# Gate/up's weight sums partly by adding DMAs, and the wide weights' pool opened during the memory heads, in a two-layer encoder

## The chip, the cores and the metric

The kernel runs on 1 core of a Trainium2 chip. The metric is the device time of one execution in microseconds (us). TensorE (PE) multiplies, VectorE (DVE) and ScalarE (ACT) work element by element, GpSimd (POOL) and SyncE (SP) mostly issue DMA transfers here. Each engine works off its own instructions in order and waits for the others by semaphores.

## The reference

x has 512 tokens of width 1024. Two layers, each with a token mixer (latent attention in layer 0, grouped-query attention in layer 1) beside four cross-attention heads into 256 memory tokens, then a SwiGLU feed-forward of width 2816. All in float32.

```python
for i in range(DEPTH):
    h = _rmsnorm(x, norm_mix[i])
    ...
    mem_out = _memory_attention(q_mem, mem_n, w_mem_kv[i], memq_norm[i], memk_norm[i])
    x = x + jnp.concatenate([mix, mem_out], axis=-1) @ w_out[i]
    x = x + _swiglu(_rmsnorm(x, norm_ffn[i]), w_gate_up[i], w_down[i])

def _swiglu(h, w_gate_up, w_down):
    gu = h @ w_gate_up
    g, u = gu[..., :D_FF], gu[..., D_FF:]
    return (jax.nn.silu(g) * u) @ w_down
```

## The kernel before, in words

**Products.** Every product is made of three TensorE passes over operands split into a high and a low part (`mm3`, L135: lines 137, 138, 139 are high x high, high x low, low x high). A weight block is loaded raw by SyncE (`load_raw`, DMA at L166), cast to its high part `whi` by ScalarE (L154), and VectorE subtracts for the low part `wlo` (L155). TensorE's L137 needs `whi`, L138 needs `wlo`.

**Gate/up.** The product h @ [gate | up] is done for 6 groups of columns (g = 0 to 4 with 512 columns, g = 5 with 256), each as a 2 x 2 block product with 7 instead of 8 multiplications (Strassen-Winograd). The two halves of the contraction and gate, up give four weight blocks b11, b12, b21, b22 (tensors w_gu, w_gl; 512 KB a tile, two tiles a block in groups 0 to 4, one in group 5). The seven products run in the order P1, P7, P2, P5, P6, P4, P3. Their weights are built in place in the raw tiles by `prep` (L794), with four VectorE subtractions of 128 x 1024 a tile, all at L792 (`tadd`): two for P7, one for P6, one for P4; 88 in the program.

```python
if p == "P1":
    src = b11
elif p == "P7":
    tadd(b11, b12, b11)
    tadd(b12, b22, b12)
    src = b12
...
elif p == "P6":
    tadd(b11, b22, b11)
```

The activations' sums (S1 to S4) are made by `sums` (L703, instructions at L707), split at L249 (ACT) and L250 (DVE) into `op` tiles. `ahead` (L820) prepares each product's weights two steps before it is multiplied (CFG LW = 2). After P1 of group g, `act_T` (L852) transposes the finished activations of group g-1 on TensorE (16 `tp` of 128 x 128, L345, into two PSUM banks), and ScalarE copies them out (`at`, L860). `post` (L862) moves results from PSUM: copies of P1's (L867) and P7's (L871) by ScalarE.

**Order.** Attention and the memory heads run as streams that `merge` (L264) interleaves by the costs they yield; one of them is `out_prefix` (L661), the first part of the output projection `w_out` (L683), which begins while the last heads run. `pipe` (L285) runs the projections' heads and tails. Weight tiles come from one pool: narrow (512 columns, 6 buffers) while attention runs, wide (1024 columns, 3 buffers) from `weight_pool(True)` on, called after the merge in L1260 and L1400. Within an engine the scheduler of the framework then fixes the final order. POOL issues 10 small transfers in the whole program (L374, L375, L379).

Of the kernel before, what the change touches and what calls it, by code (L numbers as in the profile page):

```python
# [20 lines left out]
D = 1024  # L21
# [5 lines left out]
GRID_W = 64  # L27
THETA = 10000.0

CFG = dict(mid=3, mgap=3, mdel=7, warm=9, npre=(3, 3), pre=(6, 5), WC=512, mm=3, sc=3, tp=2, norm='VA', G=33, T=9,  # L30
           W=7, WH=6, WF=3, RF=3, PR=4, delay=12, ssq='AV', ahead=1, gtag=('sc', 'mm', 'mm', 'mm'), LA=3, wlos='V',
           wloa='V', wlof='V', wlod='V', scl='V', rm='V', rad='V', hi='A', rawe='A', LW=2, tadd='V',
           r=(0.534, 0.925, 0.95, 5, 1.124, 0.86, 1.362))
# [15 lines left out]
def encoder_kernel(ctx: ExitStack, tc: tile.TileContext, a: dict, out: bass.AP):  # L49
# [235 lines left out]
    def pipe(stages, delay=None):  # L285


        pend, mid = iter(()), []

        def small_steps(n):  # L290
            for _ in range(min(n, len(mid))):
                mid.pop(0)()

        for st in stages:
            head, tail = st[0], st[-1]
            c = 0.0
# [12 lines left out]
            mid = st[1] if len(st) == 3 else []  # L309
        small_steps(len(mid))  # L310
        yield from pend

    def run(g):
# [347 lines left out]
    def out_prefix(l, acts, banks, pre, n, tag, ready):  # L661


        while not ready():
            yield None
        banks += [bank(tag) for _ in range(n)]
        for kp in range(3):
            yield from out_block(banks, range(n), acts, kp, list(w_units(a["w_out"][l, 0, kp], 512)), kp == 0, False)
        pre.append(w_early(a["w_out"][l, 0, 3], 2))

    def x_T(X, k):

# [10 lines left out]
    def w_out(l, acts, banks, pre, X, g0, early):  # L683


        sq = small(8, f"sq{l}", bufs=1)
        R = [[g4((P, 2, 512), F32, "hr") for _ in range(2)] for _ in range(2)]
        rows = [[[r[:, :, h * 256 : (h + 1) * 256] for r in R[c]] for h in range(2)] for c in range(2)]
        tmp = {}

        def scale_rows(c):
            for k in range(4):
                A.mul(R[c][k // 2][:, k % 2], x_T(X, 4 * c + k), gcol(g0 + 4 * c + k))

        def operand(src):
            res = []
            for i in range(2):
                o = g4((P, 2, 2, 256), name="op")
                split((o[:, 0], o[:, 1]), src[i])
                res.append(o)  # L700
            return res

        def sums(x, y, op):  # L703
            o = g4((P, 2, 2, 256), F32, "hs")
            o = [o[:, i] for i in range(2)]
            for i in range(2):
                op(o[i], x[i], y[i])  # L707
            return o

        def get(name):  # L710
            (a11, a21), (a12, a22) = rows
            if name == "A11":
                return operand(a11)
            if name == "S3":
                return operand(sums(a11, a21, V.tensor_sub))
            if name == "A12":
                scale_rows(1)
                return operand(a12)
            if name == "S1":
                tmp["S1"] = sums(a21, a22, V.tensor_add)  # L720
                return operand(tmp["S1"])
            if name == "S2":
                tmp["S2"] = sums(tmp["S1"], a11, V.tensor_sub)
                return operand(tmp["S2"])
            if name == "A22":
                return operand(a22)
            return operand(sums(a12, tmp["S2"], V.tensor_sub))

        n = len(banks)
        steps = [(0, kp, range(4)) for kp in range(3, 6)]  # L730
        for kp in range(6):
            steps.append((1, kp, range(4)))
            if kp < 3:
                steps.append((0, kp, range(n, 4)))
        ws = list(pre)
        bs = [banks + [bank(OTAG[t]) for t in range(n, 4)], None]
        for i, (c, kp, ts) in enumerate(steps):
            for c2, kp2, _ in steps[len(ws) : i + 1 + CFG["LW"]]:
                ws.append(list(w_units(a["w_out"][l, c2, kp2], 512)))
            if i == 0 and l == 0:  # L740
                for t in range(4):
                    X[t] = g4(dt=F32, name="x")
                    nc.sync.dma_start(X[t], a["x"][t])
            if c == 1 and kp == 0:
                bs[1] = [bank(x) for x in ("sc", "sc", "mm", "mm")]
            if i + CFG["LW"] >= len(steps):
                early(get)
            for t in ts:
                late = c == 0 and t >= n
                run(out_block(bs[c], [t], acts, kp, ws[i], kp == (3 if late else 0), kp == (2 if late else 5)))  # L750
            if (c, kp) == (0, 5):
                add_x(X, 0, bs[0], sq, range(n))
            elif (c, kp) == (0, 2):
                add_x(X, 0, bs[0], sq, range(n, 4))
            elif (c, kp) == (1, 3):
                scale_rows(0)
        add_x(X, 1, bs[1], sq, range(4))

        def stats():
            tot = small(4, "sqt")  # L760
            V.tensor_add(tot, sq[:, :4], sq[:, 4:])
            return token_rstd(tot, 4, D, f"rf{l}")[0]

        return stats

# [5 lines left out]
    def ffn(l, X, acts, banks, pre, g0, emit):  # L771
# [11 lines left out]
        def ntile(g):  # L783
            return 2 if g < 5 else 1

        def load_q(g, q):
            if g < NG:
                src = [a["w_gu"][l, g, q, i] for i in range(2)] if g < 5 else [a["w_gl"][l, q]]
                raws[g, q] = [load_raw(x, 1024) for x in src]

        def tadd(o, x, y):
            (V if eng("tadd") == "V" else GP).tensor_sub(o, x, y)  # L792

        def prep(g, p, i):  # L794
            b11, b12, b21, b22 = [raws[g, q][i] if (g, q) in raws else None for q in range(4)]
            if p == "P1":
                src = b11
            elif p == "P7":
                tadd(b11, b12, b11)
                tadd(b12, b22, b12)  # L800
                src = b12
            elif p == "P2":
                src = b21
            elif p == "P5":
                src = b11
            elif p == "P6":
                tadd(b11, b22, b11)
                src = b11
            elif p == "P4":
                tadd(b11, b21, b11)  # L810
                src = b11
            else:
                src = b22
            return wsplit(src, 1024, "wlof")

        steps = [(g, p, i) for g in range(NG) for p in PROD for i in range(ntile(g))]
        ready = {}
# [2 lines left out]
        def ahead(n):  # L820
            while nprep[0] < min(n, len(steps)):
# [1 line left out]
                if g == i == 0:  # L823
                    ops[p] = getop[0](AOP[p])
                if i == 0:
                    for q in {"P1": [1, 3], "P7": [2], "P5": []}.get(p, []):
                        if (g, q) not in raws:
                            load_q(g, q)
# [17 lines left out]
        stats = w_out(l, acts, banks, pre, X, g0, early)  # L846
        st = {}

        def two():
# [12 lines left out]
        def post(g, p):  # L862
# [9 lines left out]
            elif p == "P2":  # L872
                st["gs"] = [pr(), pr()]
                for t in range(2):
                    A.activation(st["gs"][t][:, :n], st["A"][t], AF.Silu, scale=r[:, t : t + 1])
            elif p == "P5":
                st["p5"] = two()
                for t in range(2):
# [6 lines left out]
            elif p == "P4":  # L885
                for t in range(2):
                    w, z, q = [st[x][t][:, :n] for x in ("p1", "p5", "p7")]
                    V.tensor_add(q, st["B"][t], w)
                    A.activation(q, q, AF.Silu, scale=r[:, 2 + t : 3 + t])
                    V.scalar_tensor_tensor(z, z, r[:, 2 + t : 3 + t], q, ALU.mult, ALU.mult)  # L890
            else:
                for t in range(2):
                    w, q = st["p1"][t][:, :n], st["gs"][t][:, :n]
                    V.tensor_add(w, st["C"][t], w)  # L894
                    V.scalar_tensor_tensor(w, w, r[:, t : t + 1], q, ALU.mult, ALU.mult)  # L895
# [495 lines left out]
    for h in range(4):  # L1391
# [8 lines left out]
    weight_pool(True)  # L1400

    def emit1(c):
        pass
# [96 lines left out]
```

## Time and profile before

| | |
|---|---|
| runs | 1289.7, 1290.42, 1292.85 us (median 1290.42) |
| profiled execution | 1292.64 us, of it a span of 1290.5 us |
| busy: PE / DVE / ACT / POOL | 1268.8 / 936.5 / 698.7 / 6.2 us |
| granted clock of TensorE, mean | 0.996 of full |
| HBM read / written | 119.24 / 2.10 MB |
| L792: weight sums on DVE | 88, 105.7 us in all |

Busy time is the time in which an engine has an instruction under way; idle time is told by what ended it ("<-ACT whi L154": the engine waited until ScalarE wrote whi at line 154). The granted clock is the share of TensorE's full rate (2.4 GHz) that the throttle gave; half of it is 1.2 GHz. Matmuls overlap: one of 512 columns is shown with 0.39 us while the next starts 0.23 us after it. A count such as x4 behind a timeline row puts four instructions in a row together.

### The profile page before, as it was taken

The page shows a single profiled execution, that of the slowest core. Times are in us where ns is not written, and L with a number is a line of the kernel's source. Part 1 is how long each engine was busy: PE and PEld are TensorE (multiplying, and loading weights), DVE is VectorE, ACT ScalarE, POOL GpSimd, SP SyncE. Part 2 cuts the span into 40 slices and gives each one's busy share as a digit, 9 for nine tenths or more (in the row PEclk, how much of TensorE's full clock was granted, in tenths as well). Part 3 has the DMA queues.
Part 4 walks back from the last instruction along what each step waited for, and adds up shares of the span by engine and source line. Part 5 has one row for each costly group of instructions (what it writes and reads, how often), then busy time and mean ns, then how long its engine had stood idle before and what let it go on. Part 6 is the DMA issues. An engine that isn't in the chain of part 4 may idle for free. (4 is left out here: it accounts for less than half of the span.)

```text
span 1290.5 us, 17050 instructions
## 1 busy us (share of the span) xinstructions
PE 1268.8 (98%) x6425; PEld 1061.8 (82%) x6425; DVE 936.5 (73%) x1658; ACT 698.7 (54%) x1205; POOL 6.2 (0%) x17
## 2 busy tenths in 40 slices
PE   9999999999999999999999999999998999999998
PEld 6988878988778888988888888887876888898887
DVE  6699999846978988853336898965697888896221
ACT  5587766845655455552234568865474445555110
POOL 1000000000000000000000000000000000000000
PEclk9999999999999999999999999999999999999999
DMA  7342101052323231242223212131323223216110
GB/s 227 117 141 86 34 1 66 1 213 98 115 98 131 82 131 50 88 158 66 78 99 109 81 51 86 62 129 51 115 72 141 74 106 117 79 55 237 56 62 33
DMA packets 45457, 122.43 MB, mean 95 GB/s; under 512 B 5264, under 2 KB 9872, under 8 KB 45376
## 3 DMA queue, kind: packets, MB, share of 16 engines
q1 hardware_dynamic: 44784, 119.58, 26.8%
q0 software_dynamic: 592, 1.77, 0.4%
q8 instruction: 50, 0.82, 0.2%
q14 instruction: 31, 0.25, 0.1%
HBM read 119.24 MB, written 2.10 MB: 94 GB/s over the span
## 5 line engine op out<-in xcount | busy, mean ns | idle before, releaser
L155 DVE TENSOR_TENSOR wlo<-raw,whi 128x1024 fp32r<-128x1024 f32 (+3 forms) x342 | 343.7, 1013 | 235.7 <-ACT whi L154 233.7
L154 ACT CAST whi<-raw 128x1024 fp32r<-128x1024 f32 (+3 forms) x342 | 298.8, 885 | 395.7 <-PE sc L139 262.7
L137 PE MATMUL mm<-whi,g 128*128 128x512 f32 (+3 forms) x370 | 141.2, 382 | 1.2 <-ACT whi L154 1.2
L138 PE MATMUL mm<-wlo,g 128*128 128x512 f32 (+3 forms) x370 | 139.0, 376 | 0.5 <-DVE wlo L155 0.5
L139 PE MATMUL mm<-whi,g 128*128 128x512 f32 (+3 forms) x370 | 138.0, 376 | 0.0
L138 PE MATMUL mm<-wlo,op 128*128 128x512 f32 (+1 forms) x336 | 127.8, 380 | 4.3 <-DVE wlo L155 3.9
L137 PE MATMUL mm<-whi,op 128*128 128x512 f32 (+1 forms) x336 | 126.8, 377 | 4.8 <-ACT whi L154 4.5
L139 PE MATMUL mm<-whi,op 128*128 128x512 f32 (+1 forms) x336 | 126.4, 376 | 0.0
L138 PE MATMUL sc<-wlo,op 128*128 128x512 f32 (+1 forms) x336 | 125.7, 374 | 0.0
L139 PE MATMUL sc<-whi,op 128*128 128x512 f32 (+1 forms) x336 | 125.6, 374 | 0.0
L137 PE MATMUL sc<-whi,op 128*128 128x512 f32 (+1 forms) x336 | 125.2, 373 | 0.0
L792 DVE TENSOR_TENSOR raw<-raw,raw 128x1024 f32<-128x1024 f32 x88 | 105.7, 1220 | 0.8
L138 PEld LDWEIGHTS mm<-wlo,op 128*128 128x128 f32 x336 | 63.6, 189 | 21.9 <-DVE wlo L155 11.5
L137 PEld LDWEIGHTS mm<-whi,g 128*128 128x128 f32 x370 | 69.5, 188 | 12.3 <-ACT whi L154 1.6
L138 PEld LDWEIGHTS mm<-wlo,g 128*128 128x128 f32 x370 | 69.7, 188 | 10.5 <-DVE wlo L155 1.0
L139 PEld LDWEIGHTS mm<-whi,g 128*128 128x128 f32 x370 | 69.4, 188 | 10.7 <-DVE g L246 0.2
L137 PEld LDWEIGHTS mm<-whi,op 128*128 128x128 f32 x336 | 63.6, 189 | 17.5 <-ACT whi L154 6.1
L498 PE MATMUL sc<-g,g 128*128 128x512 f32 x256 | 75.1, 410 | 0.6 <-ACT g L243 0.6
L139 PEld LDWEIGHTS sc<-whi,op 128*128 128x128 f32 x336 | 63.7, 190 | 11.2
L138 PEld LDWEIGHTS sc<-wlo,op 128*128 128x128 f32 x336 | 63.7, 190 | 11.1
L139 PEld LDWEIGHTS mm<-whi,op 128*128 128x128 f32 x336 | 63.8, 190 | 10.3
L137 PEld LDWEIGHTS sc<-whi,op 128*128 128x128 f32 x336 | 63.5, 189 | 10.6
(247 smaller groups left out, 2538.6 us busy)
## 6 DMA issues: line engine op xcount, KB each, us to landing
raw<-in_w_gu SPq DMA_DIRECT2D x80, 512.0 KB, 4.3
raw<-in_w_dn SPq DMA_DIRECT2D x44, 512.0 KB, 3.7
raw<-in_w_out SPq DMA_DIRECT2D x22, 512.0 KB, 4.4
raw<-in_w_mkv SPq DMA_DIRECT2D x32, 256.0 KB, 2.8
raw<-in_w_gin SPq DMA_DIRECT2D x30, 256.0 KB, 2.9
raw<-in_w_gl SPq DMA_DIRECT2D x8, 512.0 KB, 3.9
raw<-in_w_out SPq DMA_DIRECT2D x12, 256.0 KB, 2.5
raw<-in_w_qb SPq DMA_DIRECT2D x12, 192.0 KB, 2.4
```

The costliest lines, as they stand in the source:

```text
L137: PE.matmul(out, lhi, rhi, start=start, stop=False, skip_group_check=skip)
L138: PE.matmul(out, lhi, rlo, start=False, stop=False, skip_group_check=skip)
L139: PE.matmul(out, llo, rhi, start=False, stop=stop, skip_group_check=skip)
L154: A.copy(hi[:, :n], raw)
L155: (V if eng(kind) == "V" else GP).tensor_sub(lo[:, :n], raw, f(hi[:, :n]))
L498: PE.matmul(sc, lq[:, q * P : (q + 1) * P], rk, start=i == 0, stop=i == len(passes) - 1)
L792: (V if eng("tadd") == "V" else GP).tensor_sub(o, x, y)
```

## The change

The signs in the sums are turned so that every weight sum is an addition into its own tile, which a DMA can do: P7's weight is b12 + b22, P5's b11 + b12, P6's that plus b22, P4's that plus b21. The gate columns come out as before, the up columns negated; the operand sums (`neg_sum`) and a negated factor `r[1]` make up for it.

- P5's sum b11 += b12 is done by a DMA from HBM with addition, issued by POOL as soon as P1's weights of the same tile are split (11 a layer).
- In group 0, P7's sum b12 += b22 is done by such DMAs too (2 a layer), issued with the first loads by the new `first`, one step of `w_out` earlier than the first load was. In groups 1 to 5 VectorE adds.
- VectorE is left with 62 of 88 weight sums. The operand sums S2 and S4 become SCALAR_TENSOR_TENSOR.
- `weight_pool(True)` is now called inside `out_prefix` once the seventh attention head is done, and one more wide block of `w_out` is loaded and split there; the calls behind the merges are gone.
- `pipe` yields 2.5 (`last`) before its last tail where it has middle steps, so that in layer 0 that tail's transposes come somewhat later in the merge.

```diff
-CFG = dict(mid=3, ...
+CFG = dict(last=2.5, mid=3, ...
...
             mid = st[1] if len(st) == 3 else []
-        small_steps(len(mid))
+        if mid:
+            small_steps(len(mid))
+            yield CFG["last"]
         yield from pend
...
         pre.append(w_early(a["w_out"][l, 0, 3], 2))
+        while (l, 7) not in fin:
+            yield None
+        weight_pool(True)
+        pre.append(list(w_units(a["w_out"][l, 0, 4], 512)))
...
+        def neg_sum(o, x, y):
+            V.scalar_tensor_tensor(o, x, -1.0, y, ALU.mult, ALU.subtract)
...
-                tmp["S1"] = sums(a21, a22, V.tensor_add)
+                tmp["S1"] = sums(a22, a21, V.tensor_sub)
...
-                tmp["S2"] = sums(tmp["S1"], a11, V.tensor_sub)
+                tmp["S2"] = sums(tmp["S1"], a11, neg_sum)
...
-            return operand(sums(a12, tmp["S2"], V.tensor_sub))
+            return operand(sums(tmp["S2"], a12, neg_sum))
...
             elif (c, kp) == (1, 3):
                 scale_rows(0)
+                first()
...
-            return token_rstd(tot, 4, D, f"rf{l}")[0]
+            r, nr = token_rstd(tot, 4, D, f"rf{l}")
+
+            V.tensor_scalar_mul(nr, r, -1.0)
+            return r, nr
...
+        def dma_add(g, q, by, i):
+
+            GP.dma_start(raws[g, q][i], w_src(g, by)[i], accum_op=ALU.add)
...
-            if p == "P1":
+            if p == "P7":
+                if g > 0:
+                    V.tensor_add(b12, b12, b22)
+                src = b12
+            elif p in ("P1", "P5"):
                 src = b11
-            elif p == "P7":
-                tadd(b11, b12, b11)
-                tadd(b12, b22, b12)
-                src = b12
...
             elif p == "P6":
-                tadd(b11, b22, b11)
+                V.tensor_add(b11, b11, b22)
...
             elif p == "P4":
-                tadd(b11, b21, b11)
+                V.tensor_add(b11, b11, b21)
...
-            return wsplit(src, 1024, "wlof")
+            w = wsplit(src, 1024, "wlof")
+            if p == "P1":
+                dma_add(g, 0, 1, i)
+            return w
...
-                load_q(0, 0)
                 ahead(1)
...
+        def first():
+            load_q(0, 0)
+            load_q(0, 1)
+            for i in range(2):
+                dma_add(0, 1, 3, i)
...
-    weight_pool(True)
```

**ScalarE at the start of group 1 in layer 1.** L867 (now L888) are the copies of P1's result, L860 (L881) the `at` copies of the group before, `whi` the weight casts (P7's two, then P2's two), L871 (L892) the copies of P7's result. Before:

```order
907 L889 ACTIVATE t_9663<-t_9663,rf_2197_9686 128x512
908 L889 ACTIVATE t_9664<-t_9664,rf_2197_9686 128x512
909 L867 COPY t_9966<-mm_9924 128x512
910 L867 COPY t_9967<-sc_9925 128x512
911 L860 COPY at_9970<-tp_9971 128x512
912 L860 COPY at_9970<-tp_9977 128x512
913 L860 COPY at_9983<-tp_9984 128x512
914 L860 COPY at_9983<-tp_9990 128x512
915 L154 CAST whi_9932<-raw_9842 128x1024
916 L154 CAST whi_9950<-raw_9844 128x1024
917 L871 COPY t_10030<-mm_9996 128x512
918 L154 CAST whi_9998<-raw_9926 128x1024
```

And with the change:

```order
909 L888 COPY t_9968<-mm_9928 128x512
910 L154 CAST whi_9935<-raw_9844 128x1024
911 L888 COPY t_9969<-sc_9929 128x512
912 L154 CAST whi_9952<-raw_9846 128x1024
913 L881 COPY at_9972<-tp_9973 128x512
914 L881 COPY at_9972<-tp_9979 128x512
915 L881 COPY at_9985<-tp_9986 128x512
916 L881 COPY at_9985<-tp_9992 128x512
917 L154 CAST whi_10000<-raw_9930 128x1024
918 L154 CAST whi_10016<-raw_9932 128x1024
919 L892 COPY t_10032<-mm_9998 128x512
920 L892 COPY t_10033<-sc_9999 128x512
```

P7's two casts stand ahead of the four `at` copies now, and P2's two ahead of the copies of P7's result. Layer 0 has the first of these moves as well.

**TensorE at the same place.** L345 (now L347) are the transposes, the matmuls below them P7's first. Before, the end of the 16 transposes:

```order
4558 L345 MATMUL tp_9990<-ident,t_9595 128x128
4559 L345 MATMUL tp_9990<-ident,t_9596 128x128
4560 L345 MATMUL tp_9990<-ident,t_9783 128x128
4561 L345 MATMUL tp_9990<-ident,t_9784 128x128
4562 L137 MATMUL mm_9996<-whi_9932,op_9549 128x512
4563 L137 MATMUL sc_9997<-whi_9932,op_9549 128x512
4564 L138 MATMUL mm_9996<-wlo_9933,op_9549 128x512
```

And with the change:

```order
4555 L347 MATMUL tp_9979<-ident,t_9785 128x128
4556 L347 MATMUL tp_9979<-ident,t_9786 128x128
4557 L137 MATMUL mm_9998<-whi_9935,op_9554 128x512
4558 L137 MATMUL sc_9999<-whi_9935,op_9554 128x512
4559 L138 MATMUL mm_9998<-wlo_9936,op_9554 128x512
4560 L139 MATMUL mm_9998<-whi_9935,op_9554 128x512
4561 L138 MATMUL sc_9999<-wlo_9936,op_9554 128x512
4562 L139 MATMUL sc_9999<-whi_9935,op_9554 128x512
4563 L347 MATMUL tp_9986<-ident,t_9596 128x128
```

Six matmuls of P7 now stand between the first eight transposes and the last eight.

**ScalarE in group 5 of layer 0.** L888 copies P1's result out, L881 the `at` tiles of group 4; `whi_5568` is P5's, whose raw tile is the one that the adding DMA writes. With the change:

```order
540 L888 COPY t_5536<-mm_5506 128x256
541 L888 COPY t_5537<-sc_5507 128x256
542 L154 CAST whi_5568<-raw_5344 128x1024
543 L881 COPY at_5540<-tp_5541 128x512
544 L881 COPY at_5540<-tp_5547 128x512
545 L881 COPY at_5553<-tp_5554 128x512
546 L881 COPY at_5553<-tp_5560 128x512
```

The order here is as before; what is new is that P5's cast waits for a transfer, with the four `at` copies behind it.

## Rows read from the trace of the kernel before

**Rows 1.** Busy time of each engine over the span (share, instructions)

```profile
PE 1268.8 (98%) x6425; PEld 1061.8 (82%) x6425; DVE 936.5 (73%) x1658; ACT 698.7 (54%) x1205; POOL 6.2 (0%) x17
```

**Rows 2.** TensorE's waits by what released it: us in total, times, longest

```profile
PE mm L137 <- ACT whi L154: 7.2, 7, 1.6
PE mm L138 <- DVE wlo L155: 4.5, 8, 1.0
PE tp L345 <- DVE t L429: 2.2, 2, 1.9
```

**Rows 3.** Windows: length, busy us of PE, PEld, DVE, ACT, POOL, granted clock, DMA share, GB/s

```profile
322.60:354.90 32.30, 30.61 (x134) 24.43 (x134) 31.36 (x42) 21.47 (x29) 0.00 (x0) 1.00 0.34 115
363.00:371.20 8.20, 5.76 (x22) 4.07 (x21) 6.16 (x6) 4.95 (x8) 0.00 (x0) 0.81 0.17 32
515.00:531.00 16.00, 15.72 (x99) 13.89 (x99) 15.56 (x18) 9.43 (x14) 0.00 (x0) 1.00 0.35 126
663.00:672.00 9.00, 9.00 (x47) 7.18 (x46) 4.89 (x11) 5.13 (x13) 1.60 (x3) 1.00 0.72 249
881.60:884.70 3.10, 1.42 (x6) 0.55 (x5) 2.18 (x3) 3.05 (x4) 0.00 (x0) 1.00 0.00 0
982.00:995.50 13.50, 9.71 (x38) 6.66 (x37) 6.51 (x7) 7.05 (x12) 0.00 (x0) 0.87 0.21 78
```

**Rows 4.** Timeline, 361 to 366.4: start, us, engine, line, what, count [idle before <-releaser]

```profile
361.04 4.62 DVE L792 TENSOR_TENSOR raw<-raw,raw 128x1024 f32<-128x1024 f32 x4
...
365.26 2.00 ACT L154 CAST whi<-raw 128x1024 fp32r<-128x1024 f32 x2
...
366.36 0.50 PE L137 MATMUL mm<-whi,op 128*128 128x512 f32 x1 [1.62 <-ACT whi L154]
```

**Rows 5.** Timeline, 992 to 994.1: ScalarE and TensorE around P2 in layer 1

```profile
992.45 0.59 ACT L871 COPY t<-mm 128x512 f32<-128x512 f32 x1 [6.20 <-PE mm L139]
...
994.03 0.50 PE L137 MATMUL mm<-whi,op 128*128 128x512 f32 x1 [0.94 <-ACT whi L154]
```

**Rows 6.** Timeline, SyncE at 863 and ScalarE at 881 to 885

```profile
863.28 2.25 SPq L166 DMA_DIRECT2D raw<-in_w_out  x5
...
881.65 0.59 ACT L249 CAST g<-sc 128x512 fp32r<-128x512 f32 x1 [1.99 <-PE sc L139]
882.13 2.94 ACT L154 CAST whi<-raw 128x1024 fp32r<-128x1024 f32 x3
```

**Rows 7.** VectorE by line and shape: busy us, mean ns

```profile
L792 DVE TENSOR_TENSOR raw<-raw,raw 128x1024 f32<-128x1024 f32 x88 | 105.7, 1220 | 0.8
L895 DVE SCALAR_TENSOR_TENSOR t<-t,rf,pr 128x512 f32<-128x512 f32 x20 | 14.1, 745 | 0.0
```

**Rows 8.** POOL's issues by line (mean ns), and DMA issues: count, KB, us to landing

```profile
L374 POOL DMA_DIRECT2D g<-in_rope_gqa x1 | 0.5, 538 | 0.1
...
raw<-in_w_gl SPq DMA_DIRECT2D x8, 512.0 KB, 3.9
raw<-in_w_out SPq DMA_DIRECT2D x12, 256.0 KB, 2.5
g<-in_rope_gqa POOLq DMA_DIRECT2D x2, 256.0 KB, 4.8
```

**Rows 9.** Timeline, 518 to 529: group 5 of layer 0

```profile
518.59 1.22 DVE L155 TENSOR_TENSOR wlo<-raw,whi 128x1024 fp32r<-128x1024 f32 x1
...
526.63 1.06 ACT L154 CAST whi<-raw 128x1024 fp32r<-128x1024 f32 x1
527.98 1.07 ACT L860 COPY at<-tp 128x512 f32<-128x512 f32 x2 [0.29 <-PE tp L345]
...
527.45 0.82 PE L345 MATMUL tp<-ident,t 128*128 128x128 f32 x6
```

**Rows 10.** Timeline, 481 to 499: group 4 of layer 0

```profile
481.74 1.22 DVE L155 TENSOR_TENSOR wlo<-raw,whi 128x1024 fp32r<-128x1024 f32 x1
...
496.50 2.95 ACT L154 CAST whi<-raw 128x1024 fp32r<-128x1024 f32 x3 [0.37 <-DMA raw<-in_w_gu]
```

More of the change, by code (lines that the diff above doesn't have):

```diff
@@ L28 @@
 THETA = 10000.0
-CFG = dict(mid=3, mgap=3, mdel=7, warm=9, npre=(3, 3), pre=(6, 5), WC=512, mm=3, sc=3, tp=2, norm='VA', G=33, T=9,
+CFG = dict(last=2.5, mid=3, mgap=3, mdel=7, warm=9, npre=(3, 3), pre=(6, 5), WC=512, mm=3, sc=3, tp=2, norm='VA', G=33, T=9,
            W=7, WH=6, WF=3, RF=3, PR=4, delay=12, ssq='AV', ahead=1, gtag=('sc', 'mm', 'mm', 'mm'), LA=3, wlos='V',
@@ L681, in add_x, with w_out @@
             A.activation(tt(), xc, AF.Square, accum_out=sq[:, 4 * c + t : 4 * c + t + 1])
-    def w_out(l, acts, banks, pre, X, g0, early):
+    def w_out(l, acts, banks, pre, X, g0, first, early):
         sq = small(8, f"sq{l}", bufs=1)
@@ L784, in ntile, with w_src @@
             return 2 if g < 5 else 1
+        def w_src(g, q):
+            return [a["w_gu"][l, g, q, i] for i in range(2)] if g < 5 else [a["w_gl"][l, q]]
         def load_q(g, q):
[L787 to L792, printed above, removed]
+            if g < NG and (g, q) not in raws:
+                raws[g, q] = [load_raw(x, 1024) for x in w_src(g, q)]
+        def dma_add(g, q, by, i):
+            GP.dma_start(raws[g, q][i], w_src(g, by)[i], accum_op=ALU.add)
         def prep(g, p, i):
             b11, b12, b21, b22 = [raws[g, q][i] if (g, q) in raws else None for q in range(4)]
-            if p == "P1":
+            if p == "P7":
[3 more added lines that the diff above has]
+            elif p in ("P1", "P5"):
                 src = b11
-            elif p == "P7":
-                tadd(b11, b12, b11)
-                tadd(b12, b22, b12)
-                src = b12
             elif p == "P2":
                 src = b21
-            elif p == "P5":
-                src = b11
             elif p == "P6":
-                tadd(b11, b22, b11)
+                V.tensor_add(b11, b11, b22)
                 src = b11
             elif p == "P4":
-                tadd(b11, b21, b11)
+                V.tensor_add(b11, b11, b21)
                 src = b11
@@ L825, in ahead @@
                 if i == 0:
-                    for q in {"P1": [1, 3], "P7": [2], "P5": []}.get(p, []):
-                        if (g, q) not in raws:
-                            load_q(g, q)
+                    for q in {"P1": [1, 3], "P7": [2]}.get(p, []):
+                        load_q(g, q)
                     if p == "P6":
@@ L844, in early @@
                 ahead(2)
-        stats = w_out(l, acts, banks, pre, X, g0, early)
+        def first():
[3 more added lines that the diff above has]
+                dma_add(0, 1, 3, i)
+        stats = w_out(l, acts, banks, pre, X, g0, first, early)
         st = {}
@@ L874, in post @@
                 for t in range(2):
-                    A.activation(st["gs"][t][:, :n], st["A"][t], AF.Silu, scale=r[:, t : t + 1])
+                    A.activation(st["gs"][t][:, :n], st["A"][t], AF.Silu, scale=r[0][:, t : t + 1])
             elif p == "P5":
@@ L888, in post @@
                     V.tensor_add(q, st["B"][t], w)
-                    A.activation(q, q, AF.Silu, scale=r[:, 2 + t : 3 + t])
-                    V.scalar_tensor_tensor(z, z, r[:, 2 + t : 3 + t], q, ALU.mult, ALU.mult)
+                    A.activation(q, q, AF.Silu, scale=r[0][:, 2 + t : 3 + t])
+                    V.scalar_tensor_tensor(z, z, r[1][:, 2 + t : 3 + t], q, ALU.mult, ALU.mult)
             else:
@@ L894, in post @@
                     V.tensor_add(w, st["C"][t], w)
-                    V.scalar_tensor_tensor(w, w, r[:, t : t + 1], q, ALU.mult, ALU.mult)
+                    V.scalar_tensor_tensor(w, w, r[1][:, t : t + 1], q, ALU.mult, ALU.mult)
                 return [st["p1"][0], st["p1"][1], st["p5"][0], st["p5"][1]]
@@ L1399, in encoder_kernel @@
           (out_prefix(1, outs1, banks, out_pre, CFG["npre"][1], "mm", lambda: (1, CFG["pre"][1]) in fin and len(mvt1) == 2), 1, 0))
-    weight_pool(True)
     def emit1(c):
```

## The prediction

> **What bounds the kernel now.** I read the busy shares first: TensorE is busy 1268.8 us of the span of 1290.5, 98% [rows 1]. So no change can give much unless it removes TensorE's own work, and this one removes none of it: the products are the same 7 per column group. What can be won is TensorE's idle time, about 22 us, and the clock. The waits of TensorE come next: 7.2 us for weights cast by ScalarE (`whi`), 4.5 us for their remainders from VectorE (`wlo`), 2.2 us for a `t` tile in two places, 1.9 of them in one [rows 2]. The table by stage says where: 2.4 us idle at 363 to 371 (8.20 less 5.76 busy), 3.8 at 982 to 995, 1.7 at 881.6 to 884.7, 1.7 in the long stretch up to 354.9 where VectorE is busy 31.36 of 32.3 us [rows 3]. In the first two the granted clock is 0.81 and 0.87 as a mean: part of them ran at the lower level, 1.2 GHz, right after the idle time. That costs 0.19 x 8.2 = 1.6 us and 0.13 x 13.5 = 1.8 us on top.
>
> The timeline at 361 to 366.4 shows how the stall arises [rows 4]. It is the start of group 1, product P7. VectorE does four additions of weight blocks in 4.62 us from 361.04, so the last blocks are late; TensorE does all 16 transposes of the group before, and ScalarE copies them out (`at`) and casts P7's first block only behind these copies, at 365.26; TensorE restarts at 366.36 after 1.62 us of nothing. Layer 1 repeats this 619 us later. There P2 follows with a wait of its own: ScalarE's copy of P7's result stands in its queue ahead of P2's cast, starts at 992.45 when TensorE has finished that tile, and TensorE waits until 994.03 [rows 5].
>
> **The change part by part.**
>
> *Fewer additions on VectorE.* 88 become 62: P7 costs one addition per tile instead of two, in the first group none (a DMA adds), and P5's is added by a DMA. 26 x 1.220 us = 31.7 us of VectorE [rows 7]. VectorE is 73% busy and not the bound, so nearly all of this is hidden and counts for nothing. It counts in four kinds of places.
> (a) Group 1's start, both layers. The new order has 8 transposes, six matmuls of P7, then the other 8, and ScalarE casts P7's first block before the copies `at`. With durations from rows 4: the first addition ends at 361.04 + 1.22 = 362.3, the cast (about 1 us) at 363.4, when TensorE has just done 8 transposes; the second addition ends at 363.4 and the `wlo` 1.2 us later, at 364.6. TensorE then still waits some 0.1 + 0.7 us, against 2.4 now. I take 1.6 us of idle time and, since the remaining pause is short, the 1.6 us of clock, plus 0.4: matmul records are 0.39 us long but follow at 0.23, so each restart hides up to 0.16 us more loss than "busy" shows. Layer 0: **3.6 us**. Layer 1 holds P2's wait as well, and the new order puts P2's casts ahead of those copies: 3.8 less 0.9 left, 1.8 of clock, 0.2 of records: **4.9 us**.
> (b) The late `wlo` elsewhere. Eight waits are 4.5 us [rows 2]; four are in the windows just named (about 1.9 us), the other four, P7 of later groups, hold 2.6. Two additions fewer ahead of that `wlo` are 2.4 us; I take **1.6**.
> (c) The stretch to 354.9, group 0 of layer 0: 1.7 us idle beside a full VectorE [rows 3], four additions (4.9 us) fewer in it. The idle time hangs on operands too, which stay: **0.7**.
> The sign changes add 0.06 us each to eight operand sums (such an instruction with a scalar takes 0.745 us [rows 7], a plain one 0.68): half a microsecond of VectorE, beside TensorE; nothing, as long as (c) holds.
>
> *The pool opened during the memory heads.* In layer 1 TensorE idles 1.7 us at 881.6 to 884.7, since the casts of wide `w_out` weights come behind the last head's casts at 882.13, though the blocks were issued at 863.28 and have long been there [rows 6]. The new order casts them among the heads' work. The 1 us casts delay the heads' own casts, but ScalarE idles 2 us there [rows 6]. **1.9 us** (1.7 and the records' 0.2). The loads behind them on SP's queue change little in order, so I cost them at nothing; the cover is a raw buffer that is free some 18 us ahead.
>
> *Transposes of the last heads later* (layer 0): of `tp`'s wait for `t`, 2.2 us in two places, 1.9 lies in a place whose order is unchanged; the moved one holds 0.3 [rows 2], and with its restart **0.4**.
>
> *Added: 26 transfers of 512 KB that add, on POOL's queue.* POOL's queue is otherwise nearly empty; issuing took it 0.538 us each. What such a transfer takes no row shows. The nearest: 256 KB from POOL landed after 4.8 us, 512 KB from SP after 3.9, 256 KB from SP after 2.5 [rows 8]. So 4.8 + (3.9 - 2.5) = 6.2 us is the low bound for a plain one of 512 KB on POOL. If the add reads and writes the tile and so costs twice for every byte, 1.4 x 2 more for the whole of it: 9.0. I take 7.5, between the two. The extra traffic is 26 x 0.52 = 13.6 MB over the whole span; even at 515 to 531, where loads are dense, the transfers' share is 0.35 [rows 3]: hidden.
> In groups 1 to 4 the weight is needed late: P1's second `wlo` ends at 483.0 and P5's casts come at 496.5 and after [rows 10], so there are some 14 us and the add is hidden. In group 0 P7's transfers go out as soon as two loads are there, a step and more ahead of its cast; I cost them at nothing, covered by the operand sums of that stretch, which TensorE needs first. In group 5, with one tile, it isn't: P1's `wlo` starts 518.59 and ends 519.8; the adding transfer would land at 527.3. P5's cast stands at ScalarE ahead of the `at` copies of the group before (in the trace it starts 526.63, the copies 527.98), and TensorE's second 8 transposes wait for these copies [rows 9]. In the new order TensorE comes to them at about 527.4; the copies free a bank 1.6 us after landing (the cast, then the first copy). So the stall is landing + 1.6 - 527.4, which is 0.2 us (6.2), 1.5 (7.5) or 3.0 (9.0), in each layer: I subtract **3.0** for both, and add 0.3 for the small wait that stands there now.
> The Trainium skill, page "DMA: Bandwidth & Descriptors", section "Anatomy of one DMA", gives a DMA of this path about 2 us and its bytes at 436 GB/s, by which 512 KB would be an estimated 3.2 us. By it there would be no stall in group 5, and the sum would be 3 us better (the first rival); no run here shows such a price, and the 4.8 us of half the bytes is above it.
>
> **Sum.** 3.6 + 4.9 + 1.6 + 0.7 + 1.9 + 0.4 + 0.3 - 3.0 = 10.4 us. The profiled execution took 1292.6 us, 0.2% above the median of 1290.4: it would become 1282.2, and against the median the forecast is **1280.0 us**.
>
> **Rivals.**
> 1. *The adding transfers land within 6 us.* No stall in group 5: +3.0, and the rests in (a) may go too: 1275 to 1277. For: the plain byte time is small. Against: 4.8 us for half the size [rows 8].
> 2. *The stalls only change their releaser.* The copies and casts stand in one ScalarE queue; if P7's first cast waits for TensorE's last step and not for the addition, the pause and the half clock stay, and the gains are (c), the pool and the 0.4: 3.0, less group 5's 3.0. Result 1288 to 1290.4, no change to be measured. For: at 881 ScalarE idles for TensorE [rows 6]. Against: at 361 to 365 it is TensorE that is done first [rows 4].
> 3. *Slower: the adding transfer starts late, because POOL is held off by a busy VectorE.* At 515 to 531 VectorE is busy 15.56 of 16 us [rows 3]. If the transfer can only be set up in VectorE's gaps, it lands at 13 us or more after `wlo`. Then group 5 stalls 13 - 6.0 = 7 us in each layer, 14 for both, which is the whole gain of 13.4: about 13 us is the point from which it decides. At 16 us it is 20 - 13.4, with two falls of the clock at 1.7: +10, 1300 us. Above 14 to 16 us groups 1 to 4 would wait too. Against: the two POOL transfers at 666.5 and 667.1 were set up in 0.538 us and landed in 4.8, in a stretch where VectorE was busy 4.89 of 9 us [rows 3, 8]; but that isn't 97%.
> The Trainium skill speaks for this one: "SBUF — State Buffer", section "SBUF: two separate sides", says that GpSimd can't write the descriptors of its transfer while VectorE, in certain modes, holds a port pair that both share. The trace has no POOL transfer under a full VectorE, so it neither agrees nor differs; by a single such delay of one instruction, 1.2 us, the forecast would be 2.4 us worse, 1282.4.
> 4. *The pool does nothing* (casts placed among the heads make the heads' last product late by as much): 1.9 less, 1282.
>
> **How the numbers follow.** Forecast 0.52, rival 1 0.20, rival 2 0.13, rival 3 0.06, rival 4 0.09. What a measurement can tell from no change is 0.3%, 3.9 us: below 1286.5 or above 1294.3. Faster: the forecast and rivals 1 and 4, less 0.02 for the far end of group 5's stall: 0.79. Same: rival 2 and that end, 0.15. Slower: rival 3, 0.06. Range: from 1272 (rival 1 with the waits in (b) gone entirely) to 1289 (the bound of 9.0 us, with the clock falling at group 5 in both layers, and most of rival 2). Left out are rival 3 and the edge of rival 2, under 2 in 10.
>
> **What would show it.** Right: VectorE's weight additions 62 at 1.22 us; the windows 363 to 371 and 982 to 995 with under 1 us idle each and a clock near 1.00; no pause above 0.5 us at 881 to 885; a wait of ScalarE's `whi` for a DMA in group 5 alone, once per layer, followed by TensorE's transposes waiting for `at`; adding transfers that land in 6 to 9 us after issue. Wrong: `whi` waiting for a DMA in groups 0 to 4, landings of 13 us or more, the half clock still there after group 1's start, or TensorE idle for group 5 by over 4 us. The fall of the clock at 187 us must remain, for nothing there changes.

## The result and the profile after

The changed kernel takes **1276.36 us** (1275.37 to 1277.04, 4 runs) beside 1291.44 us of the kernel before on the same chip: ratio 0.988, 95% interval 0.987 to 0.990, 15.1 us faster. Forecast were 1280.0 with a range of 1272 to 1289 (10.4 us faster), and 1275 to 1277 as the first rival. The time is inside the range, and where the first rival put it.

The busy times of the profile after answer to [rows 1]:

```profile
PE 1262.3 (99%) x6425; PEld 1060.2 (83%) x6425; DVE 906.7 (71%) x1634; ACT 701.1 (55%) x1205; POOL 28.7 (2%) x43
```

TensorE does the same 6425 matmuls; its idle time fell from 21.7 us to 1274.6 - 1262.3 = 12.3, and its busy time by 6.5 us, which is clock and overlap, not work. TensorE's waits after, all three of [rows 2] with what is left of them:

```profile
PE mm L138 <- DVE wlo L155: 3.3, 6, 0.8
PE tp L347 <- DVE t L431: 1.9, 1, 1.9
```

The wait for `whi` (7.2 us before) is no longer in the list. Of these 7.2 us 1.5 stood in the first 20 us, in code that the change doesn't touch, and that part differs between executions of one kernel: a second profile of the changed kernel has three such waits again, 0.6 us in all. The same stretches as in [rows 3], moved by about the time gained so far, with the same columns, and as a last row group 5 of layer 1:

```profile
321.40:353.70 32.30, 31.16 (x136) 25.16 (x135) 31.43 (x40) 21.46 (x29) 0.33 (x1) 1.00 0.31 103
359.40:367.60 8.20, 7.53 (x40) 5.91 (x39) 5.03 (x5) 6.24 (x10) 0.00 (x0) 1.00 0.58 170
507.80:523.80 16.00, 15.92 (x102) 14.25 (x101) 14.07 (x17) 10.33 (x15) 0.86 (x1) 1.00 0.47 133
870.90:874.00 3.10, 3.10 (x25) 2.82 (x23) 2.08 (x5) 2.52 (x7) 0.00 (x0) 1.00 0.96 379
972.20:985.70 13.50, 12.83 (x62) 10.19 (x60) 9.19 (x9) 9.73 (x15) 0.00 (x0) 1.00 0.55 206
1119.70:1135.70 16.00, 15.93 (x102) 14.25 (x101) 14.07 (x17) 10.35 (x15) 0.86 (x1) 1.00 0.42 99
```

Group 1's start has 0.67 us of idle time in either layer (2.44 and 3.79 before), the clock is 1.00 (0.81 and 0.87), the pause at the end of layer 1's heads is gone, and group 5 has not lost: 0.08 us idle in layer 0 against 0.28, and 0.07 in layer 1, where there was none before (16.00 us busy of 16.00 at 1135.3 to 1151.3). The timeline of the start of group 1, beside [rows 4]:

```profile
358.41 2.35 DVE L814 TENSOR_TENSOR raw<-raw,raw 128x1024 f32<-128x1024 f32 x2
...
359.71 1.05 ACT L154 CAST whi<-raw 128x1024 fp32r<-128x1024 f32 x1
...
360.79 1.22 DVE L155 TENSOR_TENSOR wlo<-raw,whi 128x1024 fp32r<-128x1024 f32 x1
360.81 0.50 PE L137 MATMUL mm<-whi,op 128*128 128x512 f32 x1
...
362.07 0.50 PE L138 MATMUL mm<-wlo,op 128*128 128x512 f32 x1 [0.52 <-DVE wlo L155]
...
363.11 1.03 PE L347 MATMUL tp<-ident,t 128*128 128x128 f32 x8
```

One addition per tile, then the cast, and TensorE goes on behind its first 8 transposes; 0.52 of the 0.67 us that it waits here are for `wlo`. The adding transfers, in the profile's list of DMA issues (count, KB, median us to landing):

```profile
raw<-in_w_gu POOLq DMA_DIRECT2D x24, 512.0 KB, 5.3
...
raw<-in_w_gl POOLq DMA_DIRECT2D x2, 512.0 KB, 5.3
```

So half of them land within 5.3 us, less than the low bound of 6.2. One by one they take 5.1 to 5.8 us, but for three in group 0 of layer 1 (6.2, 6.2 and 9.8, with a transfers' share of 0.83 there), and no instruction waits for any of the 26. In group 5 of layer 0 (POOL and ScalarE, beside [rows 9]):

```profile
513.33 0.86 POOL L808 DMA_DIRECT2D raw<-in_w_gl  x1 [35.78 <-DVE wlo L155]
...
519.02 0.37 ACT L888 COPY t<-sc 128x256 f32<-128x256 f32 x1
519.28 1.05 ACT L154 CAST whi<-raw 128x1024 fp32r<-128x1024 f32 x1
520.23 1.08 ACT L881 COPY at<-tp 128x512 f32<-128x512 f32 x2
```

Issued at 513.33, landed 5.4 us later, at 518.8; P5's cast comes at 519.28 because ScalarE is busy until then. No wait for the transfer, with 0.5 us to spare. The wait of `whi` for a DMA in group 5, named as a sign that the forecast is right, isn't there.

### The profile page after: what moved, and what is told of

Read it like the earlier page. It is cut to its first block, busy times and chain, and to the rows that moved or that the text cites. A ratio compares the mean times of both kernels' runs of the same rounds, so it can differ in the third digit from the quotient of the medians.

```text
span 1274.6 us, 17121 instructions
## 1 busy us (share of the span) xinstructions
PE 1262.3 (99%) x6425; PEld 1060.2 (83%) x6425; DVE 906.7 (71%) x1634; ACT 701.1 (55%) x1205; POOL 28.7 (2%) x43
## 4 chain that ended last, share of the span: by engine, by line
PE 94%; DVE 3%; ACT 2%; DMA 0%; issue 0%; SPq 0%
PE mm L138 15%; PE mm L139 15%; PE mm L137 15%; PE sc L138 13%; PE sc L137 13%; PE sc L139 13%; PE tp L347 6%; PE sc L500 4%; DVE wlo L155 1%; ACT whi L154 1%; PE tp L566 1%; DMA raw<-in_w_cin 0%; ACT t L888 0%; DVE g L246 0%; ACT at L881 0%
## 5 line engine op out<-in xcount | busy, mean ns | idle before, releaser
L137 PEld LDWEIGHTS mm<-whi,g 128*128 128x128 f32 x370 | 69.6, 188 | 10.4 <-ACT g L243 0.7
L137 PEld LDWEIGHTS sc<-whi,op 128*128 128x128 f32 x336 | 63.3, 188 | 10.9
L139 PEld LDWEIGHTS mm<-whi,op 128*128 128x128 f32 x336 | 63.3, 188 | 10.4
L138 PE MATMUL sc<-wlo,ah 128*128 128x512 f32 x176 | 68.7, 391 | 0.0
```

Source lines behind the costliest of these rows:

```text
L137: PE.matmul(out, lhi, rhi, start=start, stop=False, skip_group_check=skip)
L138: PE.matmul(out, lhi, rlo, start=False, stop=False, skip_group_check=skip)
L139: PE.matmul(out, llo, rhi, start=False, stop=stop, skip_group_check=skip)
```

## The experiments

The theory to be tested: what the change gives is that weights are ready at a few moments (the start of group 1, the first wide `w_out` blocks), and not the 31.7 us of VectorE's time. All kernels are the changed one with one edit, unless said otherwise; ratios are to the kernel before on the same chip, where the changed kernel has 0.988 to 0.989.

**P5's sum on VectorE**, behind P1's split. (In the kernel before, its subtraction stood in P7's step.)

```diff
             if p == "P1":
-                dma_add(g, 0, 1, i)
+                V.tensor_add(b11, b11, b12)
```

> The changed kernel, but P5's weight sum is added by VectorE right after P1's split (22 more additions of 1.22 us, ahead of P7's own) and not by a DMA. Theory A (what counts is when P7's weights are ready at a group's start): P7's casts fall behind the at copies again, and most of the gain at group 1's start returns as a stall, 3.7 us in layer 0 and 5.3 with P2 in layer 1, and 0.8 for group 5: 1276.4 + 8 to 10 = 1284 to 1286. Theory B (VectorE's busy time of 27 us as such is what the DMA saves): VectorE is at 71%, so the time would rise in proportion to its full stretches only, under 3 us: 1277 to 1279, and no half clock after group 1's start. Theory C (the gain came from the pool and the rest): 1276, no change.

Measured: 1284.55 us, ratio 0.9948 (0.9933 to 0.9963): some 8 us lost, as theory A had it. (In group 0 the sum takes b12 after P7's addition, which changes what is computed there.) The clock stays at 1.00 in group 1, so the loss is idle time. It is not the one expected, though: not P7's casts but the transposes are late. TensorE's waits:

```profile
PE mm L138 <- DVE wlo L155: 7.5, 11, 0.8
PE tp L347 <- DVE t L916: 3.6, 2, 1.8
```

The rows at the start of group 1 in layer 0 (L830 are P5's additions), and one from TensorE in group 2:

```profile
355.20 1.22 DVE L830 TENSOR_TENSOR raw<-raw,raw 128x1024 f32<-128x1024 f32 x1
...
358.07 1.22 DVE L830 TENSOR_TENSOR raw<-raw,raw 128x1024 f32<-128x1024 f32 x1
...
361.60 0.75 DVE L916 SCALAR_TENSOR_TENSOR t<-t,rf,pr 128x512 f32<-128x512 f32 x1
...
362.40 0.88 PE L347 MATMUL tp<-ident,t 128*128 128x128 f32 x6 [1.77 <-DVE t L916]
...
404.79 0.50 PE L138 MATMUL mm<-wlo,op 128*128 128x512 f32 x1 [0.82 <-DVE wlo L155]
```

VectorE has P5's two additions in its queue ahead of the last steps of the finished activations `t`, which the transposes read, and ahead of P7's addition and `wlo`. The second effect is the larger: groups 2 to 4 of both layers have six new waits of 0.82 us for `wlo`, 4.9 us in all, where neither the changed kernel nor the one before has any. P5's sum is wanted much later, but in place it must be made before P7 overwrites b12. Taking b12 from HBM again lifts that order. So the 8 us are the price of these additions at this place in VectorE's queue; what they would cost in P7's step, as before, wasn't tried.

**Pool opened behind the merges again.**

```diff
-        while (l, 7) not in fin:
-            yield None
-        weight_pool(True)
-        pre.append(list(w_units(a["w_out"][l, 0, 4], 512)))
...
     X = [None] * 4
+    weight_pool(True)
```

(and the same call behind layer 1's merge)

> The changed kernel with the wide pool opened behind the merges as before, one w_out block less prepared early. Theory A (the casts of the first wide blocks came behind the last memory head's): the pause of some 2 us before the first wide w_out product of layer 1 returns, 1278 to 1279, nothing else moves. Rival (that pause only moves into the heads): within 0.5 us of 1276.4.

Measured: 1279.65 us, ratio 0.9913 (0.9897 to 0.9928): 3 to 4 us lost. The pause is back, and in the execution profiled the half clock follows it (a window of TensorE, columns as above, and two of its rows):

```profile
875.00:883.00 8.00, 6.32 (x20) 4.44 (x20) 4.19 (x4) 3.42 (x4) 0.00 (x0) 0.79 0.37 120
```

```profile
876.72 0.73 PE L137 MATMUL mm<-whi,g 128*128 128x512 f32 x2 [1.16 <-ACT whi L154]
877.98 0.77 PE L138 MATMUL mm<-wlo,g 128*128 128x512 f32 x1 [0.53 <-DVE wlo L155]
```

The idle time is 8.00 - 6.32 = 1.7 us, as in [rows 3], and 0.21 x 8 = 1.7 us of clock come on top. Two of the four runs have a mean granted clock of 0.999, like the changed kernel, and took 1279.0 and 1279.1 us; the other two, at 0.997, took 1280.2 and 1281.1. So the pause seems to cost 2 to 3 us by itself, and the clock comes on top in part of the executions.

**P7's sum by adding DMA in all groups.**

```diff
-                if g > 0:
-                    V.tensor_add(b12, b12, b22)
...
                     if p == "P3":
                         load_q(g + 1, 1)
+                        for j in range(ntile(g + 1) if g + 1 < NG else 0):
+                            dma_add(g + 1, 1, 3, j)
```

> P7's sum by adding DMA in all groups, issued when b12 is loaded: 18 additions of 1.22 us fewer on VectorE, 18 more adding transfers. Theory A (lateness of P7's weights is what remains at group 1's start, 0.5 us of wait and the restart's loss in each layer; elsewhere nothing is late): 1 to 2 us better, 1274.5 to 1275.5. Theory B (freed VectorE time pays as such): 18 x 1.22 = 22 us fewer gives as much as 26 additions did, 10 us: 1266. Rival C: the added transfers delay loads: slower than 1277.

Measured: 1280.04 us, ratio 0.9914 (0.9897 to 0.9931): slower than the changed kernel by over 3 us. Rival C holds, at one place. In groups 2 to 5 nothing changed, though VectorE does 14 additions fewer there: its time as such is worth nothing. At group 1 of layer 1 the pause shrank as theory A said (the wait for `wlo` is gone). At group 1 of layer 0 ScalarE waited for the transfers (timeline of ScalarE, the window of 19 us ahead of it, and the one behind it):

```profile
362.83 1.99 ACT L154 CAST whi<-raw 128x1024 fp32r<-128x1024 f32 x2 [6.62 <-DMA raw<-in_w_gu]
```

```profile
345.00:364.00 19.00, 17.41 (x79) 13.99 (x79) 15.33 (x22) 6.97 (x10) 3.48 (x4) 1.00 0.92 246
363.00:371.20 8.20, 5.37 (x20) 4.15 (x20) 3.58 (x3) 5.69 (x9) 0.00 (x0) 0.79 0.90 244
```

Four adding transfers stand among the loads there, the transfers' share is 0.92, and they land after 8.2 to 9.6 us. TensorE then waits 1.05 us for `whi` and 1.91 for `at`, and the half clock, which the changed kernel doesn't have there, follows. The clock is the larger part of the loss: its mean is 0.9968 over the four runs of this kernel and 0.9988 over eight of the changed one, an estimated 4.1 and 1.6 us lost.

**P5's transfer twice, one behind the other.**

```diff
             if p == "P1":
                 dma_add(g, 0, 1, i)
+                dma_add(g, 0, 1, i)
```

> P5's adding DMA is issued twice for each tile, the second waiting for the first (so P5's weight is b11 + 2 b12: this changes what is computed). It doubles the landing time behind P1's split, 5.3 to about 10.6 us. Model of the prediction: group 5 stalls landing less 6.0 us, 4.6 us in each layer, and groups 0 to 4 nothing, since they have about 14 us: 1276.4 + 9.2 = 1285.6, up to 1288.5 with a fall of the clock in both layers. Rival (P5's cast isn't what holds the transposes): under 2 us. Rival (all groups wait): over 1295.

Measured: 1311.57 us, ratio 1.0165 (1.0131 to 1.0198): far above the 1285.6 of my model. POOL's rows in group 2 say why:

```profile
394.17 0.87 POOL L808 DMA_DIRECT2D raw<-in_w_gu  x1 [30.91 <-DVE wlo L155]
399.98 1.77 POOL L808 DMA_DIRECT2D raw<-in_w_gu  x2 [4.94 <-DMA raw<-in_w_gu]
410.50 0.88 POOL L808 DMA_DIRECT2D raw<-in_w_gu  x1 [8.74 <-DMA raw<-in_w_gu]
```

POOL waits in order: the first tile's second transfer holds the second tile's first one back, the two that go out together take longer, and the last is issued 16 us after the first. So P5's second tile is there some 22 us after its split, beyond the 14 us that I had found in groups 1 to 4. It is what the slower rival describes, late transfers that stop all groups, by another cause: from group 2 on, in both layers, TensorE waits in every group.

**The same in group 5 alone**, one tile, with nothing behind it on POOL's queue.

```diff
             if p == "P1":
-                dma_add(g, 0, 1, i)
+                for _ in range(2 if g == 5 else 1):
+                    dma_add(g, 0, 1, i)
```

> P5's adding DMA issued twice in group 5 alone (its weight is then b11 + 2 b12 there: this changes what is computed), one transfer in each layer behind another; no other group's transfer is behind it on POOL's queue. Prediction's model: landing 11 us after P1's split, stall 11 - 6.0 = 5 us in each layer less the 0.6 that stands there: 1276.4 + 9 to 10 = 1286, 3 us more if the clock falls in both. Rival (the second transfer also holds something else, as it may in the run with all groups): over 1292.

Measured: 1282.39 us, ratio 0.9929 (0.9914 to 0.9944), some 5 us lost, half of what the model gave. ScalarE in group 5 of layer 0:

```profile
519.41 1.07 ACT L882 COPY at<-tp 128x512 f32<-128x512 f32 x2
524.45 1.05 ACT L154 CAST whi<-raw 128x1024 fp32r<-128x1024 f32 x1 [3.96 <-DMA raw<-in_w_gl]
525.41 1.06 ACT L882 COPY at<-tp 128x512 f32<-128x512 f32 x2
```

The cast waits 4 us for the transfer, as the landing said (513.29 to 524.4, 11.1 us). But the scheduler put the first two `at` copies ahead of the cast here, so the transposes went on and TensorE was caught later and for less. My price for a late transfer (landing less 6.0, in full) holds for the order in which the cast stands ahead of the copies, and the order itself follows the transfer.

**A plain transfer in place of the adding one.**

```diff
-            GP.dma_start(raws[g, q][i], w_src(g, by)[i], accum_op=ALU.add)
+            if q == 0:
+                GP.dma_start(raws[g, q][i], w_src(g, by)[i])
+            else:
+                GP.dma_start(raws[g, q][i], w_src(g, by)[i], accum_op=ALU.add)
```

> P5's transfers copy b12 over b11 and don't add (P5's weight is then b12: this changes what is computed). It prices the addition. If adding costs nothing in itself, a plain transfer of 512 KB on POOL's queue lands in the same 5.1 to 5.3 us. If the addition doubles the byte time, it lands in 3.9 us (1.4 less, the difference of 512 and 256 KB of SP's rows). The time of the kernel stays at 1276 in either case, since no cast waits for it.

Measured: 1277.55 us in one run, no change, as expected. The DMA list:

```profile
raw<-in_w_gu POOLq DMA_DIRECT2D x24, 512.0 KB, 3.8
raw<-in_w_gl POOLq DMA_DIRECT2D x2, 512.0 KB, 3.7
```

So POOL's queue moves 512 KB in 3.7 us (the `w_gl` rows, all of them plain), about as SP's does [rows 8], and the addition costs 5.3 - 3.7 = 1.6 us. Of these 0.3 are POOL's own issuing, 0.53 us plain and 0.86 adding.

**Group 0's sums on VectorE; no yield of 2.5.** Two small parts, each by itself.

```diff
-                if g > 0:
-                    V.tensor_add(b12, b12, b22)
+                V.tensor_add(b12, b12, b22)
...
             load_q(0, 1)
-            for i in range(2):
-                dma_add(0, 1, 3, i)
```

> The changed kernel with P7's sum of group 0 added by VectorE again (4 more additions of 1.22 us in the program's two stretches where VectorE is full). Theory A: the pause of layer 0's group 0 grows back from 1.7 to 2.5 us and layer 1's stays: 1276.4 + 0.8 = 1277.2, not to be told from no change by the median, but in the stretch. Rival (the additions delay P7's or the operands' chain in both layers): + 4 to 5 us, 1281.

Measured: 1275.38 us, ratio 0.9885 (0.9870 to 0.9901): no difference, and not even in the stretch, where the pause stayed (31.16 us busy of 32.3 at 324.4 to 356.7, as in the changed kernel). The four DMAs of group 0 give nothing.

```diff
-        if mid:
-            small_steps(len(mid))
-            yield CFG["last"]
+        small_steps(len(mid))
```

> The changed kernel without the yield of 2.5 ahead of the last tail in pipe. Theory A: the wait of 0.3 us of the transposes at 216 us returns with its restart: + 0.4 to 0.75, 1277. Rival (the later transposes shift the whole end of layer 0's heads): over 2 us, or a gain.

Measured: 1275.68 us, ratio 0.9893 (0.9878 to 0.9908): no difference to be measured. The second wait of [rows 2], 0.3 us, is back in the list, as it should be.

**The four parts undone together.** What stays of the change are the turned signs, the earlier loads in `first`, and P5's sum behind P1's split (it stood in P7's step before).

> All parts undone but the turned signs: P5's and group 0's sums on VectorE, pool opened after the merges, no yield of 2.5. If the parts add up: 1276.4 + 8.2 (P5's sum) + 3.3 (pool) + 0.8 + 0.4 = 1289, near the kernel before (1290.6), and the half clock returns in group 1. If the signs or the order of the sums alone gave something: 1285 or less.

(The edit is the four above together.) Measured: 1287.91 us, ratio 0.9980 (0.9969 to 0.9992, 12 runs). Added up in ratios, P5's sum costs 0.9948 - 0.9883 = 0.0065, the pool 0.0030, the other two 0.0012 as measured, 0.0107 in all; undone together they cost 0.0097. So the parts add up within their intervals. What stays is worth some 2.6 us (1.0 to 4.0 by the interval), with 88 additions as before; which of the three things gives it wasn't tried. Group 1's windows of this kernel, and a row of group 2:

```profile
358.80:367.00 8.20, 6.43 (x35) 4.75 (x34) 7.78 (x10) 4.46 (x7) 0.00 (x0) 1.00 0.00 0
977.90:991.40 13.50, 11.21 (x55) 8.49 (x55) 9.64 (x11) 7.77 (x12) 0.00 (x0) 1.00 0.40 145
```

```profile
406.56 0.50 PE L138 MATMUL mm<-wlo,op 128*128 128x512 f32 x1 [0.82 <-DVE wlo L155]
```

1.8 and 2.3 us idle, and no half clock in this execution. Before, 2.4 and 3.8, with it. Against that, groups 2 to 4 have the six waits of 0.82 us of the first experiment, which the kernel before doesn't have: the 2.6 us are what is left of a larger gain. Most of them are clock: its mean is 0.9984 over these 12 runs and 0.9966 over 31 of the kernel before, an estimated 2.0 and 4.3 us lost.

**A mixture, and the changed kernel beside it.** Group 0's sums on VectorE, and P7's sum of group 1 by DMA in layer 1 alone.

```diff
-                if g > 0:
+                if (l, g) != (1, 1):
                     V.tensor_add(b12, b12, b22)
...
                         load_q(g + 1, 1)
+                        if (l, g) == (1, 0):
+                            for j in range(2):
+                                dma_add(1, 1, 3, j)
...
             load_q(0, 1)
-            for i in range(2):
-                dma_add(0, 1, 3, i)
```

> P7's sum of group 0 by VectorE in both layers (which cost nothing in the run before), and P7's sum of group 1 by adding DMA in layer 1 alone, where it took the pause at the group's start from 1.4 to 0.6 us, and not in layer 0, where four adding transfers among six loads landed too late. If pauses alone count: 0.8 us better than the changed kernel, 1275.5, within what a measurement can tell; if the transfers saved (2 fewer) or VectorE's time counted, it would show a difference of over 2 us.

> The changed kernel itself, as the measure for the two beside it on the same chip: 1276, ratio 0.988 to 0.989 to the kernel before.

Measured: the mixture 1276.0 us, ratio 0.9879 (0.9863 to 0.9896); the changed kernel 1277.8, 0.9892 (0.9877 to 0.9906). The intervals overlap: whether the mixture is better stays open. It is no worse, with 2 adding transfers fewer.

## Why the prediction was right, and where not

The direction and most of the places were right; the sum came out 3.6 us short (1280.0 for 1276.4), and 4.7 short as a gain over the kernel before on the same chip (10.4 for 15.1). Term by term, from the windows above and [rows 3]:

| term | forecast, us | measured, us |
|---|---|---|
| (a) group 1, layer 0 | 3.6 | 1.8 idle + 1.6 clock = 3.4 |
| (a) group 1, layer 1 | 4.9 | 3.1 idle + 1.8 clock = 4.9 |
| (b) late `wlo` elsewhere | 1.6 | 0.2, which stands in (c)'s stretch and counts there |
| (c) group 0, layer 0 | 0.7 | 0.5 |
| pool, layer 1 | 1.9 | 1.7, and 3 to 4 when undone alone |
| later transposes | 0.4 | 0.3 |
| group 5, both layers | -2.7 | 0.2 - 0.1 = +0.1 |

**(a) was right**, in the size and in the order of events that it rested on; that P5's additions, where VectorE makes them, take the room, the first experiment shows. What it left out: with all four parts undone, part of the pause and the half clock were gone already. And its clock terms are those of one execution. Worked out from the mean granted clocks, the kernel before loses 4.3 us to the clock and the changed one 1.6: 2.7 us on the average, where (a) counts 3.4.

**(b) was wrong in its place.** The forecast said that "the other four, P7 of later groups, hold 2.6"; the trace of before, row by row, has these waits elsewhere. Two of the four stand in group 0 of layer 0 and two in that of layer 1 (0.98, 0.36, 0.79 and 0.35 us), and groups 2 to 4 had none. So two of them lay in the very stretch that (c) counted. I had only the sum of a list and no rows for its parts. After the change these four are 0.79, 0.35, 0.79 and 0.35. Here is one of before, from TensorE's timeline:

```profile
345.58 0.51 PE L138 MATMUL mm<-wlo,op 128*128 128x512 f32 x1 [0.98 <-DVE wlo L155]
```

**(c)** had about its size, by another cause: without group 0's DMAs the stretch is the same, so it is not P7's four additions that were in the way. Two waits make up the half microsecond: one of 0.35 us for `whi`, at 343.87 before, is gone in the kernel with the four parts undone too, so what stays there removes it; the row above fell from 0.98 to 0.79, and is 0.98 again only where all four are undone together.

**The pool** was right in place and idle time. Its worth depends on whether the half clock follows the pause: it didn't in the profile of the kernel before and did in that of the kernel that undoes the pool alone.

**Group 5 is the term that was mis-sized**, by 2.8 us. "256 KB from POOL landed after 4.8 us" was taken as the price of POOL's queue. It wasn't: the rows of 4.8 us stand in a stretch with a transfers' share of 0.72 [rows 3], and 512 KB plain take 3.7. The trace of before had a quiet row to compare: a POOL transfer of 128 KB landed after 2.2 us at 615 us (share 0.11 over 612 to 620), and one of the same kind after 4.7 us at 666, beside those of 4.8. I took 7.5; the landings were 5.4 and 5.3, and below 6.0 nothing waits. The low bound failed because it was built on rows under load. The addition's price of 1.6 us is near the 1.4 that I derived for twice the bytes, once and not twice as I counted it.
The page of the Trainium skill weighed there ("DMA: Bandwidth & Descriptors", section "Anatomy of one DMA") gave an estimated 3.2 us: near the 3.7 of a plain transfer, 2.1 below the adding one. By its consequence, no stall, it was the better guide; of the addition's price it says nothing there.

**The rivals.** The first came true. The second fell: P7's first cast now starts at 359.71, as its addition is done, and the pause shrank from 2.44 to 0.67 us. The third, that a busy VectorE holds POOL off, fell too. One transfer of group 2 was on its way from 392.67 to 397.90, and VectorE was busy for all of that time:

```profile
392.67:397.90 5.23, 5.23 (x25) 4.33 (x24) 5.23 (x8) 2.11 (x2) 1.71 (x2) 1.00 0.70 112
```

Its issue took 0.86 us and it landed after 5.2. So what the page "SBUF — State Buffer" of the Trainium skill (section "SBUF: two separate sides") warns of doesn't appear with the instructions under way there (TENSOR_TENSOR and SCALAR_TENSOR_TENSOR of float32). Its other half, that a late transfer would stop all groups, is real: doubled landing times behind one another on POOL's queue cost 35 us. The fourth fell with the pool's 3 us.

The table's terms hold 10.9 of the 15.9 us between the two spans. A further 1.5 are in the first 20 us, where TensorE is busy 17.01 us before and 18.49 after, in code that the change doesn't touch, so this belongs to the execution profiled. The rest, about 3.5 us, is in no term; that it is the overlap at each restart, which busy times can't show, is likely but not shown.

So the size was in part luck. The terms add up to 10.9 us for a forecast of 10.4 because group 5, 2.8 us better, makes up for (b), which gave nothing of its own. And the time falls on the first rival's number by the 4 to 5 us that no term holds: group 5's stall is absent, as that rival says, but the rests in (a) that it had going too are still there.

## What to carry to other kernels

Count freed time of an engine for nothing, and look for the few moments at which its queue holds back something that TensorE needs next: 22 additions of a weight wanted some 14 us later cost 8 us where they stood ahead of what was wanted at once, and 14 others nothing. Recomputing in place forces an order; reading the source again by an adding DMA lifts it, at 1.6 us more than a plain transfer. It stays hidden as long as nobody wants the tile before it lands (here after 5.1 to 5.8 us, under dense loads up to 9.8) and no second transfer waits behind it on the same queue. And price a queue from a quiet row: the landing built on rows under load was 2 us too long, and made a stall of 3 us where there was none.

## What was not expected of the hardware

The half clock doesn't follow a pause each time. The same pause of 1.9 us at 184 us stands in all these kernels, and the window of 180 to 192 us shows (the kernel before, the one with all parts undone, the one with P7 by DMA):

```profile
180.00:192.00 12.00, 9.55 (x43) 7.56 (x43) 10.12 (x33) 5.14 (x11) 0.00 (x0) 0.86 0.00 0
```

```profile
180.00:192.00 12.00, 9.76 (x39) 7.53 (x38) 9.39 (x31) 4.74 (x10) 0.00 (x0) 0.72 0.00 0
```

```profile
180.00:192.00 12.00, 9.55 (x58) 7.85 (x57) 11.68 (x39) 6.65 (x14) 0.00 (x0) 1.00 0.01 1
```

So 0 to 3.4 us hang on a pause of one length, and which it will be can't be read from the pause, nor from the program: the changed kernel has 0.86 there, and up to that place its instructions are those of the third. What decides it wasn't tried. A pause's price is better given with and without the clock, as two numbers.
